# Grouping the state products of a state space stage: 512 moving columns instead of 256, and the stream sums added by accumulating transfers

## The chip, the cores and the metric

The kernel runs on one core of a Trainium2 chip. The metric is the device time of one execution in microseconds (us). The kernel before takes 2615.48 us (median of three runs, 2615.11 to 2616.11). All times below are of that core. PE is the matmul engine and PEld its weight load, DVE the vector engine, ACT the scalar engine, POOL the general engine, and SP the engine whose queue issues most of the loads.

## The reference

One layer for 256 frames of a new stream (the "prompt") and 16 frames for each of 8 running streams, so 384 rows in all, in float32. The part the change touches is the state space branch (64 heads of 64 columns in 8 groups, state size 128 per head):

```
xbc, new_conv = causal_conv(xbc, st_conv, conv_w, conv_b)      # 4 taps, SiLU
h, ys: per chunk
    y = einsum(cb * decay, xdt) + einsum(C, h) * exp(cum)      # C times the stored state
    h = h * exp(last) + einsum(B, w_end, xdt)                  # new state = decayed state + B x
a_ssd = gated_rmsnorm(y + d_skip * xh, z, ssd_norm)            # RMS over each group of 512 columns
```

Outputs are the two blocks of y and the new states; `new_ssm_prompt` (4 KB times 512, 2 MB) comes from the prompt product, `new_ssm_sample` (16 MB) is, per stream, the stored state times its decay plus the stream's own sum B x.

## The kernel before, in words

The whole kernel is one list of matmuls on PE. Every projection streams its weights from HBM: SP loads a 128x1024 block `w` (512 KB), ACT rounds it to the high part `wh` (line 72), DVE subtracts to get the low part `wl` (line 73), and PE does three matmuls of 384 columns for each of 8 blocks of the contraction (lines 100 to 102: `wh` by the high part of the activations, `wh` by their low part, `wl` by the high part). One such block is called a half here: 24 matmuls. A projection is two halves. `w`, `wh` and `wl` have three buffers each, so a half's split can begin only when PE has finished the half three places earlier, and it must end before PE comes to it.

The stage of the change (pools `phd` and `phd1`, from line 564) runs over 8 groups. A group has ten projections in this order: `BT`, `CT`, and four convolution inputs (all called `pj_x` in the profile), then four gates `z0` to `z3` (`pj_z`). Between the projections stand two blocks of small matmuls, called lumps here: the x lump after the third convolution input, and the z3 lump after `z3`. A group's 512 columns are worked on in two pairs of 256 columns; the x lump does the inner products of the first pair and the sums of the previous group's second pair, the z3 lump the other half. In a lump (names as in the profile):

- `t_pp` (line 693, `py<-xhl,Bhl`): the prompt's new state, six matmuls of 256 columns per pair. Its result shares a PSUM bank with `yi`, is copied by ACT (`pe`) and written.
- `t_trx` (650), `t_cb` (640), `t_trB` (634), `t_yT` (671): transposes and C B.
- `t_Y` (679): the outputs within the chunk, 48 rows of the trace per pair.
- `t_yi` (658, `py<-hs,Cm`): C times the stored states `hs`, eight matmuls of 256 columns per pair, shown as 16.
- `t_su` (798): B x of each stream, eight matmuls of 256 columns per pair. DVE then adds the result to the decayed `hs` (line 807, 64 adds), and one POOL transfer of 1 MB writes `new_ssm_s`.

Around the lumps ACT and DVE do the rest of the stage in their own order, mixed with the weight splits: the taps and SiLU of the convolution (`cbuf`, `cacc`, `xs`), the decay factors `E` (`eside`, exponentials and line 780), `hs` times its decay (`dside`), the gate `zs` (line 928), and the norm of the previous group (`final`, `finish`). For the norm ACT squares (`ysq`), POOL adds into `ssum` (line 836, one `ysq` buffer), ACT and DVE split the sum into `nh_g` and `nl_g` (lines 188, 189), and PE spreads it over the partitions by two matmuls with ones (`bc_g`, lines 192 and 193), which stand between `z1` and `z2`. ACT loads a function table (`ACT_TABLE_LOAD`) whenever the next function is not in the loaded one; exponentials and the SiLU functions alternate.

The order on each engine is set by a scheduler when the program is built. `lump` and `chain` only pin the order of PE's blocks; `later()` puts an instruction behind the last weight split. Engines run their lists strictly in order. After the stage come the last gate projections `gb` (their second half lies in this stage's end), with reloads `ar` of the branch's result (SP, line 966), which ACT and DVE split into `abh` and `abl` for the next stage's projections `sp`.

At the program's start SP loads the inputs `xw` in blocks; ACT and DVE split each into `xgh` and `xgl` and its first weights into `wh_e` and `wl_e`, and PE's first projection `pj_p` follows the arrivals.

## Time and profile before

| what | value |
|---|---|
| median of three runs | 2615.48 us |
| profiled execution | 2615.75 us, of which the span on the page is 2613.8 us |
| PE busy | 2602.6 us, 100% of the span |
| DVE, ACT, POOL busy | 1775.5, 1302.2, 185.7 us |
| PE's waits in the whole span | 1.2 us and 0.9 us, one each |
| granted clock of PE | 1.00 |
| state space stage | about 450 to 1205 us, one group every 90.0 us |

Busy shares are to be read with care here: matmuls overlap in the profile (a 384-column matmul is shown as 0.33 us long and the next one starts 0.163 us later), so what a block of matmuls takes is read from start to start. In rows of the trace in order of time the columns are: start (us from the span's start), length of the merged rows (us), engine, line, operation, result and sources, shape, count, and in brackets the idle time of the engine before, with what ended it.

### The profile page before, as it was taken

What the parts mean: (1) busy time and instruction counts of PE and PEld (TensorE: products, weight loads), DVE (VectorE), ACT (ScalarE), POOL (GpSimd) and SP (SyncE); (2) the same over time, 40 slices, a digit from 0 to 9 for tenths busy, and PEclk for the clock granted to TensorE, in tenths of its full rate; (3) what the DMA queues carried; (4) which work ended last, traced back from release to release, by engine and by line L of the source; (5) the groups of instructions that cost most, each with busy time, mean ns of one, the idle gap of its engine ahead of it and who ended that gap; (6) DMA issues with size and microseconds to landing.
All of it is one profiled execution on the core that took longest, in us unless ns stands there. A gap on an engine that the chain in (4) does not pass through costs nothing.

```text
span 2613.8 us, 40314 instructions
## 1 busy us (share of the span) xinstructions
PE 2602.6 (100%) x16001; PEld 2506.4 (96%) x16001; DVE 1775.5 (68%) x2383; ACT 1302.2 (50%) x1981; POOL 185.7 (7%) x264
## 2 busy tenths in 40 slices
PE   9999999999999999999999999999999999999998
PEld 9999999999999999999999988999999999999997
DVE  6685334788888888876434434766676868677677
ACT  6443325566566566744332334645454545454454
POOL 0000000001111111121000000000000000000000
PEclk9999999999999999999999999999999999999999
DMA  7444446566766676666654555533443444344343
GB/s 284 143 136 155 149 147 203 179 206 209 230 210 223 197 241 201 218 218 226 211 161 157 158 193 169 208 138 130 142 132 129 159 156 143 140 145 138 137 145 137
DMA packets 139421, 457.76 MB, mean 175 GB/s; under 512 B 17569, under 2 KB 44769, under 8 KB 125793
## 3 DMA queue, kind: packets, MB, share of 16 engines
q1 hardware_dynamic: 117120, 326.98, 39.0%
q0 software_dynamic: 22112, 128.21, 13.4%
q8 instruction: 126, 2.06, 0.3%
q14 instruction: 63, 0.51, 0.1%
HBM read 410.26 MB, written 44.86 MB: 174 GB/s over the span
## 4 chain that ended last, share of the span: by engine, by line
PE 98%; ACT 1%; DVE 1%; issue 0%; DMA 0%; POOL 0%; ACTq 0%; POOLq 0%
PE pj_up L100 6%; PE pj_up L101 6%; PE pj_up L102 6%; PE pj_x L100 4%; PE pj_x L102 4%; PE pj_x L101 4%; PE pj_sp L102 3%; PE pj_z L102 3%; PE pj_z L101 3%; PE pj_sp L100 3%; PE pj_sp L101 3%; PE pj_z L100 3%; PE X L1401 2%; PE c L1401 2%; PE X L1399 2%; PE c L1400 2%
## 5 line engine op out<-in xcount | busy, mean ns | idle before, releaser
L100 PE MATMUL pj_up<-x1h,wh_up 128*128 128x384 f32 (+1 forms) x1024 | 334.2, 326 | 0.0
L102 PE MATMUL pj_up<-x1h,wl_up 128*128 128x384 f32 (+1 forms) x1024 | 333.9, 326 | 0.0
L101 PE MATMUL pj_up<-x1l,wh_up 128*128 128x384 f32 (+1 forms) x1024 | 333.9, 326 | 0.0
L100 PE MATMUL pj_x<-xgh,wh_x 128*128 128x384 f32 x768 | 252.2, 328 | 0.0
L102 PE MATMUL pj_x<-xgh,wl_x 128*128 128x384 f32 x768 | 250.8, 327 | 0.9 <-DVE wl_x L73 0.9
L101 PE MATMUL pj_x<-xgl,wh_x 128*128 128x384 f32 x768 | 250.6, 326 | 0.0
L72 ACT ACTIVATE wh_up<-w_up 128x1024 fp32r<-128x1024 f32 x126 | 133.1, 1056 | 189.3 <-PE pj_up L101 114.7
L101 PEld LDWEIGHTS pj_up<-x1l,wh_up 128*128 128x128 f32 x1024 | 193.7, 189 | 0.4
L100 PEld LDWEIGHTS pj_up<-x1h,wh_up 128*128 128x128 f32 x1024 | 193.7, 189 | 0.4
L102 PEld LDWEIGHTS pj_up<-x1h,wl_up 128*128 128x128 f32 x1024 | 193.7, 189 | 0.0
L73 DVE TENSOR_TENSOR wl_up<-w_up,wh_up 128x1024 fp32r<-128x1024 f32 x126 | 153.7, 1220 | 57.9 <-ACT wh_up L72 57.0
L102 PE MATMUL pj_z<-xgh,wl_z 128*128 128x384 f32 x512 | 167.0, 326 | 0.0
L100 PE MATMUL pj_z<-xgh,wh_z 128*128 128x384 f32 x512 | 167.0, 326 | 0.0
L102 PE MATMUL pj_sp<-abh,wl_sp 128*128 128x384 f32 x512 | 167.0, 326 | 0.0
L101 PE MATMUL pj_z<-xgl,wh_z 128*128 128x384 f32 x512 | 167.0, 326 | 0.0
L100 PE MATMUL pj_sp<-abh,wh_sp 128*128 128x384 f32 x512 | 167.0, 326 | 0.0
L101 PE MATMUL pj_sp<-abl,wh_sp 128*128 128x384 f32 x512 | 167.0, 326 | 0.0
L73 DVE TENSOR_TENSOR wl_sp<-w_sp,wh_sp 128x1024 fp32r<-128x1024 f32 x64 | 78.3, 1224 | 116.6 <-ACT wh_sp L72 116.6
L72 ACT ACTIVATE wh_x<-w_x 128x1024 fp32r<-128x1024 f32 x96 | 101.0, 1052 | 107.1 <-PE pj_z L101 53.0
L73 DVE TENSOR_TENSOR wl_x<-w_x,wh_x 128x1024 fp32r<-128x1024 f32 x96 | 117.3, 1221 | 51.5 <-ACT wh_x L72 51.5
L72 ACT ACTIVATE wh_sp<-w_sp 128x1024 fp32r<-128x1024 f32 x64 | 67.8, 1059 | 166.3 <-PE pj_sp L101 158.2
L100 PEld LDWEIGHTS pj_x<-xgh,wh_x 128*128 128x128 f32 x768 | 145.3, 189 | 2.6 <-issue 0.4
(459 smaller groups left out, 7112.0 us busy)
## 6 DMA issues: line engine op xcount, KB each, us to landing
w_up<-w_up SPq DMA_DIRECT2D x128, 512.0 KB, 3.5
w<-w_dn POOLq DMA_DIRECT2D x60, 1024.0 KB, 5.2
w_x<-w_in SPq DMA_DIRECT2D x96, 512.0 KB, 4.1
w_z<-w_in SPq DMA_DIRECT2D x64, 512.0 KB, 3.6
w_sp<-w_ssd SPq DMA_DIRECT2D x64, 512.0 KB, 3.5
w_ga<-w_ga SPq DMA_DIRECT2D x32, 512.0 KB, 3.5
w_pp<-w_pp SPq DMA_DIRECT2D x32, 512.0 KB, 3.5
hs<-ssm POOLq DMA_DIRECT2D x16, 1024.0 KB, 6.8
```

The source lines that it names most:

```text
L72: cut[0] = s.activation(h, w, AF.Copy)
L73: cut[1] = v.tensor_tensor(l, w, h.bitcast(F32), ALU.subtract)
L100: te.matmul(out, wh, xh, start=first, stop=False, **how)
L101: te.matmul(out, wh, xl, start=False, stop=False, **how)
L102: return te.matmul(out, wl, xh, start=False, stop=last, **how)
L1399: te.matmul(o, h[:, t], vh, start=go, stop=False, skip_group_check=True)
L1400: te.matmul(o, h[:, t], vl, start=False, stop=False, skip_group_check=True)
L1401: last[0] = te.matmul(o, l[:, t], vh, start=False, stop=False, skip_group_check=True)
```

## The change

What was done for a pair of 256 columns is done for a group of 512:

- `t_pp`: six matmuls of 512 columns for a group, all in the x lump of the next group, in a PSUM bank of their own; one copy `pe` of 512 columns and one transfer of 256 KB instead of two of 128 KB.
- `t_yi`: eight matmuls of 512 columns for a group, all in its x lump; `hs` lies in two tiles of four streams each, loaded at the group's start, and `yis` is one operation of 512 columns (`yside`).
- `t_su`: two sets of four matmuls of 512 columns (`state(D, 0)` in the next x lump, `state(D, 1)` in the next z3 lump). The result is no longer added to `hs` by DVE. The decayed `hs` is written as it is (`dside`), and the sums are copied by ACT into `sst`, one of four copies behind each of the four halves after the lump (`spill`), and added to the written states in HBM by a transfer with `accum_op=ALU.add`.
- Buffers: `xst`, `sst`, `hs`, `Bhl`, `BT`, `CT` one each, `xs` five; the constant `ones` goes; `dynamic_dma_scratch_size=4096`.

```diff
@@ proj
             half(o, q, take(src, f"{name}_{q}"), rhs)
             if hook:
                 hook()
+            if spill:
+                with later():
+                    spill.pop(0)()
@@ pload, t_yi, t_pp
-        def pload(S):
-            S.hs = pd.tile([P, NB, 2 * P], F32, tag="hs", name=f"hs{S.nm}")
-            gp.dma_start(S.hs, io["ssm"][S.qd])
+        def pload(D):
+            D.hs = []
+            for k in range(2):
+                hs = pd.tile([P, 4, 512], F32, tag=f"hs{k}", name=f"hs{D.g}_{k}", bufs=1)
+                gp.dma_start(hs, io["ssm"][D.g, :, 4 * k : 4 * k + 4])
+                D.hs.append(hs)
...
-        def t_pp(S, py):
-            S.pp = py[:, :256]
+        def t_pp(D):
+            D.pp = mmtile(f"pp{D.g}")
...
+        def prompt(D):
+            lump(lambda: t_pp(D))
+            pe = pd.tile([P, 512], F32, tag="pe", name=f"pe{D.g}", bufs=1)
+            s.copy(pe, D.pp)
+            gp.dma_start(io["new_ssm_p"][D.g], pe)
@@ dside, state
+        def dside(D, k):
+            hs = D.hs[k].rearrange("p b (h q) -> p b h q", h=8)
+            dec = decb[:, D.g * 8 : D.g * 8 + 8, 4 * k : 4 * k + 4].rearrange("p h b -> p b h")
+            v.tensor_tensor(hs, hs, dec.unsqueeze(3).to_broadcast([P, 4, 8, 64]), ALU.mult)
+            gp.dma_start(io["new_ssm_s"][D.g, :, 4 * k : 4 * k + 4], D.hs[k])
+
+        def state(D, k):
+            su = []
             def t_su():
-                hs = S.hs.rearrange("p (r h) n -> p h r n", h=2)
-                for r2 in (0, 2):
...
-                        v.tensor_tensor(hr, hr, su[h].rearrange("p (r n) -> p r n", r=2), ALU.add)
+                for r in range(2):
+                    for h in range(2):
+                        t = slice(h * 64, h * 64 + 64)
+                        su.append(sstile(f"su{D.g}_{k}_{r}_{h}"))
+                        i = te.matmul(su[-1], D.bs[t, 2 * k + r, :], D.xst[t, 2 * k + r, :], start=True, stop=True)
                 return i
             lump(t_su)
-            gp.dma_start(io["new_ssm_s"][S.qd], S.hs)
+            sst = pd.tile([P, 4, 512], F32, tag="sst", name=f"sst{D.g}_{k}", bufs=1)
+            def out(i):
+                s.copy(sst[:, i], su[i])
+                if i == 3:
+                    gp.dma_start(io["new_ssm_s"][D.g, :, 4 * k : 4 * k + 4], sst, accum_op=ALU.add)
+            spill.extend([lambda i=i: out(i) for i in range(4)])
@@ the loop over groups, in the x lump
-            S.py = mmtile(f"py{S.nm}")
             if g:
-                lump(lambda: t_pp(prev.p[1], S.py))
+                prompt(prev)
...
-            lump(lambda: t_yi(S))
+            lump(lambda: t_yi(D))
             xside(S)
+            yside(D)
             mside(D)
             if g:
-                state(prev.p[1])
+                state(prev, 0)
@@ behind the z3 projection
-            lump(lambda: t_pp(S, S1.py))
             lump(lambda: t_trx(S1))
             lump(lambda: t_yT(S))
             lump(lambda: t_Y(S))
-            lump(lambda: t_yi(S1))
             xside(S1)
-            state(S)
+            if g:
+                state(prev, 1)
             final(S)
+            stack(D)
```

The scheduler gives the built program another order at three places that the prediction speaks of. In the rows a name's last number tells the tile apart; `wh_z_2_0` is the high part of the weights of the first half of `z2`, and a row without a result, `ACT_TABLE_LOAD`, loads a function table.

**ACT and PE between `z1` and `z2`** (third group of the loop; the other groups read alike). ACT before, from the split for the second half of `z1`:

```order
L72 ACTIVATE wh_z_1_1_7703<-w_z_1_1_7701 128x1024
L779 ACTIVATE E_0_7658<-E_0_7658 128x2x256
L188 ACTIVATE nh_g_7811<-ssum_7054 128x384
L593 COPY cbuf_4128<-cstate 128x8x3
L593 COPY cbuf_4130<-cstate 128x8x3
L607 ACT_TABLE_LOAD
L607 ACTIVATE xs_7656<-cacc_7651,vec 128x384
L928 ACTIVATE zs_0_7731<-zs_0_7731 128x384
L72 ACTIVATE wh_z_2_0_7750<-w_z_2_0_7748 128x1024
L72 ACTIVATE wh_z_2_1_7780<-w_z_2_1_7778 128x1024
```

and with the change, from the last of the four copies into `sst`, which stands right behind the split of the second half of `z1`:

```order
L819 COPY sst_0_7434<-su_0_1_1_7432 128x512
L609 ACT_TABLE_LOAD
L609 ACTIVATE xs_7525<-cacc_7520,vec 128x384
L794 ACT_TABLE_LOAD
L794 ACTIVATE E_0_7527<-E_0_7527 128x2x128
L936 ACT_TABLE_LOAD
L936 ACTIVATE zs_0_7603<-zs_0_7603 128x384
L795 ACT_TABLE_LOAD
L795 ACTIVATE E_0_7527<-E_0_7527 128x2x256
L71 ACTIVATE wh_z_2_0_7620<-w_z_2_0_7618 128x1024
L71 ACTIVATE wh_z_2_1_7650<-w_z_2_1_7648 128x1024
L190 ACTIVATE nh_g_7681<-ssum_6922 128x384
```

Two exponentials of `E` have moved behind the convolution's SiLU (`xs`) and around the gate's (`zs`), with a table load before each of the four, and `nh_g` has moved from behind the split of `z1` to behind both splits of `z2`. In the stretch from the x lump to `z2` ACT has seven table loads per group instead of four. On PE the two matmuls that use `nh_g` and `nl_g` stood together ahead of `z2`; with the change the rows from the last matmul of `z1` are:

```order
L101 MATMUL pj_z_1_7617<-xgh_495,wl_z_1_1_7574 128x384
L194 MATMUL bc_g_7685<-nh_g_7681,onesr 128x384
L99 MATMUL pj_z_2_7711<-xgh_230,wh_z_2_0_7620 128x384
L100 MATMUL pj_z_2_7711<-xgl_231,wh_z_2_0_7620 128x384
L195 MATMUL bc_g_7685<-nl_g_7682,onesr 128x384
L101 MATMUL pj_z_2_7711<-xgh_230,wl_z_2_0_7621 128x384
```

The first stays ahead of `z2` and the second has moved behind two of its matmuls.

**ACT at the program's start.** Before, the splits of the first inputs followed each other (`xgh`, `wh_e`, and so on); with the change:

```order
L273 ACTIVATE xgh_252<-xw_182,x0g 128x384
L295 ACTIVATE wh_e_249<-xw_182 128x256
L595 COPY cbuf_4118<-cstate 128x8x3
L595 COPY cbuf_4120<-cstate 128x8x3
L595 COPY cbuf_4122<-cstate 128x8x3
L273 ACTIVATE xgh_270<-xw_185,x0g 128x384
L297 ACTIVATE wh_e_274<-xw_185 128x512
```

Three copies of the state space stage's first convolution inputs have moved up to between the second and the third block of inputs. They need the transfer `cstate<-state_conv` (648 KB), which was issued by POOL at about 422 us and is now POOL's first transfer, behind its memsets and with nothing to wait for.

**SP behind the stage.** Before, with `ar` the reloads and `w_gb` the weights of the last gate projections:

```order
L65 DMA w_gb_1_12563<-w_gb 128x1024
L966 DMA ar_12798<-a_scr_72 128x384
L966 DMA ar_12804<-a_scr_73 128x384
L966 DMA ar_12840<-a_scr_74 128x384
L966 DMA ar_12846<-a_scr_75 128x384
L65 DMA w_gb_0_12598<-w_gb 128x1024
```

and with the change:

```order
L64 DMA w_gb_1_12715<-w_gb 128x1024
L973 DMA ar_12525<-a_scr_72 128x384
L973 DMA ar_12531<-a_scr_73 128x384
L973 DMA ar_12567<-a_scr_74 128x384
L973 DMA ar_12573<-a_scr_75 128x384
L64 DMA w_gb_0_12762<-w_gb 128x1024
L973 DMA ar_12614<-a_scr_76 128x384
```

The first four reloads have moved behind ten more weight blocks (before they were issued at 1170.7 us), and the first of them now also waits for the last accumulating transfer of `sst`, whose memory it takes.

More of the change, by code (lines that the diff above doesn't have):

```diff
@@ L49, in build @@
     ident = cst[:, C_IDENT : C_IDENT + P]
-    ones = cst[:, C_ONES : C_ONES + P]
     def mmtile(name):
@@ L115, in half @@
         last[0] = ins
-    queue, ready = [], []
+    queue, ready, spill = [], [], []
     def take(src, name):
@@ L203, in build @@
     b_scr = [dram.tile([P, 2, P], F32, name=f"b_scr{i}") for i in range(G)]
-    x_scr = [dram.tile([P, 2, 2, P], F32, name=f"x_scr{i}") for i in range(16)]
+    x_scr = [dram.tile([P, 2, 4, P], F32, name=f"x_scr{i}") for i in range(G)]
     x1_scr = [dram.tile([P, DM], F32, name=f"x1_scr{b}") for b in range(3)]
@@ L867, in build @@
                 eside(prev.p[1], 1)
-                dside(prev.p[1])
                 for i in range(4):
                     gate_b(i, pd, "cacc")
-                py = mmtile("pp_last")
-                lump(lambda: t_pp(prev.p[1], py))
+                prompt(prev)
                 lump(lambda: t_yT(prev.p[1]))
                 lump(lambda: t_Y(prev.p[1]))
-                state(prev.p[1])
+                state(prev, 0)
                 final(prev.p[1])
-                for i in range(4, 8):
+                for i in range(4, 6):
+                    gate_b(i, pd, "cacc")
+                state(prev, 1)
+                for i in range(6, 8):
                     gate_b(i, pd, "cacc")
@@ L936, in build @@
                 finish(prev)
+            dside(D, 0)
             zproj(2)
-            dside(S)
+            dside(D, 1)
             cload(D.p[1])
```

115 lines of the change are left out of this document (46 added, 69 removed).

## The prediction

> **What bounds the kernel now.** I read the page first, then PE's waits.
>
> ```profile
> span 2613.8 us, 40314 instructions
> PE warm_o L234 <- DVE warm L230: 1.2, 1, 1.2
> PE pj_x L102 <- DVE wl_x L73: 0.9, 1, 0.9
> ```
>
> PE stands still for 2.1 us in the whole span. So a microsecond saved on PE is a microsecond of the end, and a microsecond that PE waits anywhere is one too: nothing later can give it back. The question for every part of the change is whether PE's list gets shorter, and whether something PE needs now comes late. The next view is the busy time of each engine in one stretch of the stage, from an x lump to the norm's matmuls ahead of `z2` (columns: stretch, its length, then busy time and instruction count of PE, PEld, DVE, ACT, POOL, then clock, DMA share, GB/s).
>
> ```profile
> 635.00:666.00 31.00, 31.00 (x248) 29.79 (x247) 27.34 (x38) 24.48 (x48) 4.66 (x5) 1.00 0.68 228
> ```
>
> DVE has 3.7 us to spare here and ACT 6.5. Over the whole span both have plenty, but in this stretch work for ACT is nearly on the path, because the weight splits and `nh_g` stand in its list behind the rest.
>
> **PE's own work.** The lump rows in order of time, the first matmul after the lump, and the norm's first matmul:
>
> ```profile
> 635.49 0.88 PE L693 MATMUL py<-xhl,Bhl 128*128 128x256 f32 x6
> 636.21 0.82 PE L650 MATMUL trx<-cst,xs 128*128 128x128 f32 x6
> ...
> 640.14 1.08 PE L658 MATMUL py<-hs,Cm 128*32 128x256 f32 x16
> 641.15 0.75 PE L798 MATMUL su<-xst,bst 64*128 64x256 f32 x8
> 641.83 0.43 PE L100 MATMUL pj_x<-xgh,wh_x 128*128 128x384 f32 x1
> 665.34 0.34 PE L192 MATMUL bc_g<-nh_g,onesr 128*128 128x384 f32 x1
> ```
>
> From 641.83 to 665.34 lie six halves of 24 matmuls of 384 columns: 23.51 / 144 = 0.163 us each, so 512 columns take about 0.163 x 4/3 = 0.217 us. Six prompt matmuls of 256 columns take 0.72 us, 1.44 a group; six of 512 take 1.30. The 16 rows of `yi` run as four column groups at once, four rounds of 0.217 and 0.14 besides, 1.01 a pair and 2.02 a group; one set of 512 columns is four rounds of 0.434 and 0.14, 1.88. `su` is 0.68 a pair, four rounds of about 0.11 and 0.24 around them, 1.36 a group; two sets with two rounds of 0.217 and 0.2 around them make 1.27. Together 0.37 us less per group. Against it, in the z3 lump `yi` no longer stands between `Y` and `su`, so `Y` is followed by another tiling directly; I take 0.1 us for it. Eight groups, and one more lump at the end: about **-1.8 us**. Bounds: -0.5 (the fixed parts come back in full) and -4 (they vanish with the instructions). The columns streamed are the same; only fixed parts can go, so this term is small whatever happens.
>
> **ACT between the x lump and z2.** The change moves the state sums from DVE (64 adds) to ACT (64 copies), and the new order has seven table loads in this stretch of a group where there were four. Here every instruction of ACT's list counts. Rows of before, same group:
>
> ```profile
> 640.22 0.85 ACT L750 ACTIVATE xhl<-xdw 128x768 fp32r<-128x768 f32 x1 [1.46 <-DVE xdw L736]
> 641.09 1.28 ACT L768 ACT_TABLE_LOAD   x1
> 642.38 0.40 ACT L768 ACTIVATE E<-cbc,tok 128x128 f32<-128x128 f32 x1
> ...
> 643.23 0.69 ACT L770 ACTIVATE E<-cbc,tok 128x128 f32<-128x128 f32 x2
> 643.83 0.39 ACT L768 ACTIVATE E<-cbc,tok 128x128 f32<-128x128 f32 x1
> ...
> 645.00 0.41 ACT L778 ACTIVATE E<-E 128x256 f32<-128x256 f32 x1
> 645.30 0.62 ACT L779 ACTIVATE E<-E 128x512 f32<-128x512 f32 x1
> 645.82 0.39 ACT L768 ACTIVATE E<-cbc,tok 128x128 f32<-128x128 f32 x1
> 646.12 0.51 ACT L835 ACTIVATE ysq<-zs 128x384 f32<-128x384 f32 x1
> 646.53 1.05 ACT L72 ACTIVATE wh_z<-w_z 128x1024 fp32r<-128x1024 f32 x1
> 647.48 0.98 ACT L770 ACTIVATE E<-cbc,tok 128x128 f32<-128x128 f32 x3
> ...
> 654.56 0.24 ACT L594 COPY cbuf<-cbuf 128x45 f32<-128x45 f32 x1
> ...
> 655.36 1.05 ACT L72 ACTIVATE wh_z<-w_z 128x1024 fp32r<-128x1024 f32 x1
> ...
> 656.83 0.51 ACT L188 ACTIVATE nh_g<-ssum 128x384 fp32r<-128x384 f32 x1
> ...
> 660.14 0.52 ACT L928 ACTIVATE zs<-zs 128x384 f32<-128x384 f32 x1 [0.65 <-DVE zs L927]
> 660.57 1.99 ACT L72 ACTIVATE wh_z<-w_z 128x1024 fp32r<-128x1024 f32 x2
> ```
>
> From start to start: `xhl` 0.87, a table load 1.29, an `E` of 128 columns 0.30, the exponential pair 0.30 + 0.52 = 0.82, `ysq` 0.41, a split 0.95, the convolution's three (654.56 to 655.36) 0.80, `zs` 0.43; `xs`, of the same size, 0.5. A copy into `sst` is in no row. Its floor is the 0.30 of a 256-column operation, its ceiling the 0.62 of a 512-column one; I take 0.47, near the 0.52 at which the 512-column row lets the next one start.
>
> With the change the list from `xhl` to `nh_g` is: `xhl` 0.9, 7 table loads 9.0, 16 `E` 4.8, 2 exponential pairs 1.6, 2 `ysq` 0.8, 4 `sst` 1.9, 5 splits (`z0_1` to `z2_1`) 4.8, the convolution's three 0.8, 2 `xs` 1.0, `zs` 0.4, `nh_g` 0.5: **26.5 us without one wait**. `xhl` starts 4.7 us into the lump (640.22 - 635.49); the longer prompt product need not move that, since DVE is at a split until then. So `nh_g` is ready no sooner than 31.2. PE comes to `bc_g` after a lump of 6.34 + 0.58 (prompt) + 0.87 (`yi`) - 0.04 = 7.75 and six halves of 23.5: at **31.25**. Before, `nh_g` was ready at 21.9 (656.83 + 0.51 - 635.49) and PE used it at 29.85: a cover of 8 us that is now zero before any wait is counted.
>
> There are waits. The second `ysq` needs the only buffer, which POOL's add frees:
>
> ```profile
> 601.75 4.70 POOL L836 TENSOR_TENSOR ssum<-ssum,ysq 128x384 f32<-128x384 f32 x1 [0.75 <-ACT ysq L835]
> 646.71 1.05 POOL L836 TENSOR_TENSOR ssum<-ssum,ysq 128x384 f32<-128x384 f32 x1 [0.97 <-ACT ysq L835]
> 649.82 2.01 POOL L836 TENSOR_TENSOR ssum<-ssum,ysq 128x384 f32<-128x384 f32 x1 [2.06 <-ACT ysq L835]
> ```
>
> Before, six `E` and a split stood between the two `ysq`; now only a `sst` copy and one `E`, 0.8 us. By the middle duration ACT waits 2.01 + 0.1 + 0.05 - 0.8, about 1.4 us (0.4 by the shortest, 4 by the longest), and 0.6 before the first `ysq`, whose gate product DVE finishes about 8 us into the lump. So `nh_g` is ready at about 33.2: PE waits **2.0 us** at `bc_g`. Behind it DVE's list decides:
>
> ```profile
> 649.76 1.21 DVE L780 TENSOR_TENSOR E<-E,cbm 128x1024 f32<-128x1024 f32 x1
> 660.02 0.55 DVE L189 TENSOR_TENSOR nl_g<-ssum,nh_g 128x384 fp32r<-128x384 f32 x1
> 661.64 2.36 DVE L73 TENSOR_TENSOR wl_z<-w_z,wh_z 128x1024 fp32r<-128x1024 f32 x2 [1.07 <-ACT wh_z L72]
> ```
>
> The last exponential ends 2.4 us (two splits and `nh_g`) before `nh_g`, at 30.8; then come 1.21 for `E`, 2.36 for the two low parts and 0.55 for `nl_g`, ready at 35.0. PE, having passed two matmuls of `z2`, would be at the second `bc_g` at 33.2 + 0.5 = 33.7 and waits another **1.3**. So 3.4 us per group, and seven groups have a previous one: **+24 us**. Bounds: with no wait inside ACT's list 1.4 us per group, +10; with POOL's longest add and `sst` at 0.62 about 6.6, +46. What follows in a group has time to recover, as ACT waits for PE's buffers from `z3` on, so the wait does not grow from group to group.
>
> On the table loads the Trainium skill speaks against the change still more: "ScalarE: Activation LUTs", "What ACT_TABLE_LOAD costs", gives 1283 ns for the load and about 1380 ns of drain, 2.66 us a switch. The trace has the 1.28, but the next instruction starts 1.29 us after the load began, so there is no drain here; by the page, as an estimate, each group would lose some 10 us more.
>
> **The opening.** POOL now sends 648 KB at once into the time in which the inputs arrive:
>
> ```profile
> 5.00:10.00 5.00, 5.00 (x27) 4.95 (x27) 3.53 (x8) 3.26 (x7) 0.00 (x0) 1.00 1.03 397
> cstate<-state_conv POOLq DMA_DIRECT2D x1, 648.0 KB, 7.5
> 10.97 0.62 ACT L271 ACTIVATE xgh<-xw,x0g 128x384 fp32r<-128x384 f32 x1 [0.52 <-DMA xw<-xw]
> 13.43 0.33 PE L101 MATMUL pj_p<-xgl,wh_e 128*128 128x384 f32 x1
> 13.84 0.43 PE L102 MATMUL pj_p<-xgh,wl_e 128*128 128x384 f32 x1
> ```
>
> The DMA share is 1.03 at 397 GB/s, so 648 KB (664 thousand bytes) more put the inputs behind it back by 1.6 us. PE already waited for the block that came at 10.97 (a step of 0.41 instead of 0.16), so the delay is paid in full. The three copies ahead of `xgh` in ACT's list wait for the same transfer: issued at about 1 us and 7.5 us under way, it lands at 8.5, 0.2 us a copy, about as late as the delayed input. **+1.6 us**, bounds 0.5 (the transfer fills gaps) and 4 (it lands later, and ACT with it).
>
> **Behind the stage.** The first reloads `ar` now stand ten weight blocks later in SP's list, and ACT's list has splits of `gb` behind `abh`, which wait for them.
>
> ```profile
> new_ssm_s<-hs POOLq DMA_DIRECT2D x16, 1024.0 KB, 5.0
> hs<-ssm POOLq DMA_DIRECT2D x16, 1024.0 KB, 6.8
> ar<-a_scr SPq DMA_DIRECT2D x32, 192.0 KB, 4.5
> ```
>
> Each reload takes 4.5 us to land; with two or four of them ahead of a split, and two halves (7.8 us) between its release and its use, one or two splits of `gb12` come 1 to 2 us late: **+3 us**, bounds 0 and 9. SP comes to the first `ar` about 11 us after the last accumulating transfer is issued. That transfer is in no row: at least the 5.0 of the plain write, at most, if it reads and writes one after the other, 11.8. I take 8, which hides.
>
> **Sum**, against the profiled execution's own 2615.75 us (0.3 above the median): 2615.75 - 1.8 + 24 + 1.6 + 3 = **2643**.
>
> **Rivals.** *ACT keeps up* (not slower): POOL's add takes its short 1.05 and the copies 0.3, and the overlaps on ACT are a little better than my sum; then the waits at `bc_g` vanish and -1.8 and +1.6 remain: 2615.5. It speaks for it that ACT had 6.5 us free in the stretch; against it that three loads, four copies and the new wait take 3.9 + 1.9 + 2.0 = 7.8, and that it takes off only the part of ACT's list that is in front of the last exponential, while DVE's tail of 4.1 us stays. *A partial form*, 1.4 us a group or less: 2620 to 2630. *The accumulating transfer is slow*: from 11 us on, the first `ar` holds SP, with the weight blocks behind it; at 20 us the end moves by 20 - 11 = 9 and about 4 for the reloads behind it: 2656. Nothing in the trace excludes it. *The clock falls*: PE now stands 2.0 and 1.3 us, nearly at a stretch, in each of seven groups. If the clock were halved for the half behind each, 3.9 us more per group: 2643 + 27 = 2670. The granted clock was 1.00 in all stretches I looked at, but none had a wait over 1.2 us. The Trainium skill, "TensorE: Matmul & The Clock Gate", Part 1, has the clock fall after an idle window of about 3.4 us; two matmuls lie between the waits, so by that rule it could go either way.
>
> **How the numbers follow.** Forecast 0.64 (its own range 2630 to 2656), partial 0.10, ACT keeps up 0.06, slow transfer 0.11, clock 0.09. The range 2626 to 2662 leaves out ACT keeping up, the clock, and a part of the partial and slow-transfer cases. A measurement of this kernel tells about 0.2% (5.2 us) from no change. Slower by more: everything but ACT keeping up and the edge of the partial case, 0.93; within 0.2%: 0.04; faster: 0.03, only if ACT keeps up and PE's fixed parts vanish.
>
> **What would show it.** Right: PE's waits list `bc_g` on ACT's `nh_g` and on DVE's `nl_g`, seven times each, 2 and 1.3 us, and the groups take about 93 us instead of 90.0; ACT is busy nearly all the time from the x lump to `z2`. PE's first projection ends 1 to 2 us later; `pj_gb` waits for `wh_gb` once or twice. Wrong: no wait at `bc_g`, or a wait at a weight split elsewhere in the stage; a granted clock under 1; `ar` waiting for `sst`.

## The result, and the profile after

The changed kernel takes **2662.5 us** (median of six, 2660.0 to 2667.5); the kernel before took 2615.9 on the same chip. The ratio is **1.018**, 95% interval 1.0169 to 1.0195: slower, as forecast, but by 46.6 us where 27 were expected; the forecast was 2643 and its range ended at 2662. The profiled execution took 2662.4 us, 2660.7 of it inside the span.

First PE's waits on the page of the kernel after (total us, times, longest):

```profile
span 2660.7 us, 39759 instructions
PE bc_g L194 <- ACT nh_g L190: 9.0, 7, 1.5
PE bc_g L195 <- DVE nl_g L191: 5.7, 7, 0.9
PE su L812 <- DVE xdw L746: 4.8, 8, 1.6
PE pj_p L313 <- ACT xgh L273: 3.2, 1, 3.2
PE pj_gb L99 <- ACT wh_gb L71: 1.1, 1, 1.1
PE pj_x L99 <- ACT wh_x L71: 1.1, 1, 1.1
```

The two waits at `bc_g` are there, seven times each. The third row, `su` behind DVE's eviction `xdw`, was in no forecast. Now one group in the order of time, ACT, DVE and PE around the norm:

```profile
576.94 1.28 ACT L936 ACT_TABLE_LOAD   x1
...
578.78 1.28 ACT L795 ACT_TABLE_LOAD   x1
...
580.61 1.99 ACT L71 ACTIVATE wh_z<-w_z 128x1024 fp32r<-128x1024 f32 x2
582.50 0.51 ACT L190 ACTIVATE nh_g<-ssum 128x384 fp32r<-128x384 f32 x1
583.07 0.45 PE L194 MATMUL bc_g<-nh_g,onesr 128*128 128x384 f32 x1 [1.19 <-ACT nh_g L190]
584.15 0.55 DVE L191 TENSOR_TENSOR nl_g<-ssum,nh_g 128x384 fp32r<-128x384 f32 x1
584.75 0.69 PE L195 MATMUL bc_g<-nl_g,onesr 128*128 128x384 f32 x1 [0.91 <-DVE nl_g L191]
585.24 0.52 PE L101 MATMUL pj_z<-xgh,wl_z 128*128 128x384 f32 x1
585.55 0.53 PE L99 MATMUL pj_z<-xgh,wh_z 128*128 128x384 f32 x1
...
588.24 0.33 PE L99 MATMUL pj_z<-xgh,wh_z 128*128 128x384 f32 x1
```

ACT has no idle time from 576.94 to 583.0: two table loads with the gate and an exponential behind them, two splits, then `nh_g`. PE stands 1.19 us for it, runs two matmuls, stands 0.91 us for `nl_g`, and after that each matmul of 384 columns takes 0.32 us from start to start, twice the usual 0.163, until the last row. The same place in stretches (length, busy time and count of PE, PEld, DVE, ACT, POOL, clock, DMA share, GB/s):

```profile
580.00:584.70 4.70, 2.65 (x15) 2.05 (x13) 3.97 (x5) 3.22 (x7) 0.55 (x1) 0.99 1.09 257
584.70:588.20 3.50, 3.45 (x11) 3.45 (x12) 1.02 (x2) 0.00 (x0) 0.00 (x0) 0.52 0.97 356
588.20:591.70 3.50, 3.50 (x24) 3.50 (x23) 0.81 (x1) 1.89 (x2) 0.00 (x0) 1.00 1.00 414
```

The granted clock falls to 0.52 for one stretch and returns. PE counts as busy all the while, so the waits list does not show this loss; the start-to-start steps do. Up to the end of PE's work there are nine such patches, some 87 matmuls at half speed, which cost 13.5 us. The profile also shows the lump behind `z3`, where the new wait for `su` stands, and what came before it on ACT and DVE:

```profile
970.84 1.06 ACT L71 ACTIVATE wh_z<-w_z 128x1024 fp32r<-128x1024 f32 x1 [6.54 <-DMA w_z<-w_in]
971.93 1.23 DVE L72 TENSOR_TENSOR wl_z<-w_z,wh_z 128x1024 fp32r<-128x1024 f32 x1 [5.37 <-ACT wh_z L71]
...
981.26 0.82 PE L655 MATMUL trx<-cst,xs 128*128 128x128 f32 x6
...
982.27 2.35 DVE L72 TENSOR_TENSOR wl_x<-w_x,wh_x 128x1024 fp32r<-128x1024 f32 x2
984.10 0.50 PE L812 MATMUL su<-xst,bst 64*128 64x512 f32 x2
985.48 0.54 DVE L746 TENSOR_TENSOR xdw<-trx,tok 128x384 f32<-128x384 f32 x1
986.17 0.46 PE L812 MATMUL su<-xst,bst 64*128 64x512 f32 x1 [1.56 <-DVE xdw L746]
```

The third `su` needs the PSUM bank in which the transposes `trx` lie until DVE has evicted them (`xdw`), and DVE comes to it late. The chain begins at a late weight block: ACT stands 6.54 us until `w_z` has landed, DVE 5.37 us for ACT's split of it, and from 971.93 on DVE works without a pause, two weight splits of 2.35 us at the end, until it reaches `xdw`. Start to start these lumps take 3.5 to 6.3 us, 8.6 us over seven times 3.50. Last the transfers of after (KB each, median us to landing), three of them as they were before, and the opening of after in the order of time:

```profile
new_ssm_s<-sst POOLq DMA_DIRECT2D x16, 1024.0 KB, 11.6
hs<-ssm POOLq DMA_DIRECT2D x16, 1024.0 KB, 8.7
w_x<-w_in SPq DMA_DIRECT2D x96, 512.0 KB, 5.2
w_z<-w_in SPq DMA_DIRECT2D x64, 512.0 KB, 4.4
xw<-xw SPq DMA_DIRECT2D x1, 320.0 KB, 7.6
```

```profile
w_x<-w_in SPq DMA_DIRECT2D x96, 512.0 KB, 4.1
w_z<-w_in SPq DMA_DIRECT2D x64, 512.0 KB, 3.6
xw<-xw SPq DMA_DIRECT2D x1, 320.0 KB, 4.2
```

```profile
1.31 0.67 POOL L570 DMA_DIRECT2D cstate<-state_conv  x1 [0.36 <-issue]
9.30 0.61 ACT L273 ACTIVATE xgh<-xw,x0g 128x384 fp32r<-128x384 f32 x1 [4.69 <-DMA xw<-xw]
9.97 0.92 PE L313 MATMUL pj_p<-xgh,wh_e 128*128 128x384 f32 x4 [3.25 <-ACT xgh L273]
```

The accumulating transfer takes 11.6 us. `w_x` and `w_z` land 1.1 and 0.8 us later than before, and ACT's waits for `w_z`, which the list of before does not show at all, come to 41.8 us. At the start the second block of inputs (320 KB) landed 3.4 us later than before, and PE stood 3.25 us for it.

All of it, from start to start on PE, in the two profiled executions (spans 2613.8 and 2660.7, a difference of 46.9):

| where | forecast | measured |
|---|---|---|
| PE's own small matmuls | -1.8 | -0.8 |
| waits at `bc_g`, seven groups | +24 | +19 |
| opening | +1.6 | +4.0 (1.5 of it at half clock) |
| late weights at the start of the stage and in `gb` | +3 | about +3.6 |
| waits at `su`, z3 lumps | 0 | +8.6 |
| half clock outside the opening | 0 (a rival) | +12.0 |
| sum | +26.8 | +46.4 |

From `sp` on the two kernels take the same time. The stretch from the stage's first matmul to `sp`'s, called the stage below, went from 846.9 to 889.6 us.

### The profile page after: what moved, and what is told of

Read it like the earlier page. It is cut to its first block, busy times and chain, and to the rows that moved or that the text cites. A ratio compares the mean times of both kernels' runs of the same rounds, so it can differ in the third digit from the quotient of the medians.

```text
span 2660.7 us, 39759 instructions
## 1 busy us (share of the span) xinstructions
PE 2624.0 (99%) x15761; PEld 2509.4 (94%) x15761; DVE 1736.7 (65%) x2311; ACT 1367.9 (51%) x2065; POOL 172.8 (6%) x272
## 3 DMA queue, kind: packets, MB, share of 16 engines
q0 software_dynamic: 24288, 144.99, 16.3%
## 4 chain that ended last, share of the span: by engine, by line
PE 94%; DVE 3%; ACT 1%; DMA 1%; issue 1%; POOL 0%; SPq 0%; DVEq 0%; ACTq 0%
PE pj_up L99 6%; PE pj_up L100 6%; PE pj_up L101 6%; PE pj_x L99 5%; PE pj_x L101 5%; PE pj_x L100 5%; PE pj_sp L100 3%; PE pj_sp L99 3%; PE pj_sp L101 3%; PE pj_z L99 2%; PE pj_z L101 2%; PE pj_z L100 2%; PE X L1408 2%; PE c L1408 2%; PE c L1406 2%; PE X L1407 2%
## 5 line engine op out<-in xcount | busy, mean ns | idle before, releaser
L101 PEld LDWEIGHTS pj_x<-xgh,wl_x 128*128 128x128 f32 x768 | 146.0, 190 | 1.0 <-DVE wl_x L72 1.0
```

What stands on the lines that cost most here:

```text
L101: return te.matmul(out, wl, xh, start=False, stop=last, **how)
```

## The experiments

The theory: ACT's list got seven table loads per group instead of four, because the copies into `sst` changed the scheduler's order, and so `nh_g` and the splits of `z2` come late; idle PE then loses its clock. The rivals: the copies themselves, the accumulating transfer, the larger loads and the opening.

**The opening undone.** `cstate` is queued behind `mlast`, the last write of the stage before into `ma_scr`.

```diff
-        gp.dma_start(cst_, io["state_conv"])
+        with behind(mlast[0]):
+            gp.dma_start(cst_, io["state_conv"])
```

> The changed kernel with one edit: the transfer of the stored convolution states is queued on POOL behind the last write of the pool branch, so that it and its three copies on ACT leave the opening. Theory (the transfer holds the input blocks up, and ACT and PE behind them): PE's first projection loses its 3.2 us wait and the cold matmuls behind it, the first gate projection starts at 53.0 us instead of 57.0, and the whole is 4.0 us shorter, about 2658.5. The state space stage keeps its seven waits at bc_g. Rival (the opening is slow for another reason, such as a longer load of the program): the 4 us stay.

Measured 2658.3 us, 1.016 (1.0143 to 1.0177): 4.2 less than the change. `pj_ga` begins at 53.7 instead of 57.0, and the waits at `bc_g` and `su` stay (9.1, 6.0 and 5.1). So the time came out as the theory said (2658.5): the opening costs 3 to 4 us and nothing else hangs on it.

**The factors early.** `eside(S, 1)` is written ahead of `zproj(0)`; copies, accumulating transfer and opening stay.

```diff
-            zproj(0)
             eside(S, 1)
+            zproj(0)
```

> The changed kernel with one line moved: the second half of the decay factors of a group's first pair is written ahead of the projection z0 instead of behind it. ACT's list then has four table loads between the x lump and z2 instead of seven; the 64 copies on ACT, the accumulating transfers and the opening stay. Theory (ACT's list with its table loads makes nh_g and the split of z2 late, and the clock falls behind the waits): the waits at bc_g vanish, by the rows' durations about 0.8 us per group remain at a split of z1, and the clock falls seldom; the part from the first convolution projection to the first pj_sp takes 847 (before) + 7 + up to 5 = 854 to 862 us, the whole 2630 to 2638. Rival one (the 64 copies on ACT alone make it late, whatever the tables): waits of 2 us or more per group stay, the whole above 2645. Rival two (the accumulating transfers slow the weights' loads): the whole stays at 2655 to 2662.

Measured 2630.5 us, 1.0054 (1.0039 to 1.0069), within the 2630 to 2638 of the theory. Between 545 and 1100 us ACT has 36 table loads (60 with the change, 38 before), no wait at `bc_g` is left, and no patch of half clock in the stage. So the order of ACT's list, and not the time of the copies, made the waits at `bc_g`: with the patches behind them and what they pushed, 32 us. Waits at `su` remain (2.5 us), and 14 us over the kernel before.

**The norm's split early.** All seven table loads stay; only `nh_g` and `nl_g` move ahead of `z0`.

```diff
+            if g:
+                prev.hl = norm_split(pd, prev.ssum, f"g{prev.g}")
             zproj(0)
             eside(S, 1)
```

> The changed kernel with the split of the norm's sum (nh_g on ACT, nl_g on DVE) written ahead of the projection z0, so that both stand well ahead of the splits of z2. ACT still has seven table loads per group in this stretch. Theory (the length of ACT's list is what counts, the place of nh_g only says which wait shows it): no wait at bc_g, in its place a wait of about 2 us per group at the splits of z2; 13 us less than that for the bc_g waits saved at most; the whole 2645 to 2658. Rival (the place of nh_g is the cause): no waits over 0.5 us in the groups, the whole at 2625 or less.

Measured 2644.2 us, 1.0109 (1.0094 to 1.0125), 18 less than the change and just below the 2645 to 2658 expected. The wait moved, as PE's waits show:

```profile
PE pj_z L99 <- ACT wh_z L71: 6.6, 7, 1.0
PE pj_z L101 <- DVE wl_z L72: 6.0, 7, 0.9
```

PE now waits for the splits of `z2`, behind which `nh_g` had stood. So the late work is the whole list up to `z2`; `nh_g` was only the last of it: the waits were 14.7 us at `bc_g` and are 12.6 here. The rest of what the move brought lies behind the waits. In the profiled execution (2648.2 us) three patches of half clock are left outside the opening instead of eight, and the z3 lumps take 3.7 us over seven times 3.50 instead of 8.6.

**The copies on DVE.** ACT's list then has four table loads again.

```diff
-                s.copy(sst[:, i], su[i])
+                v.tensor_copy(sst[:, i], su[i])
```

> The changed kernel with the 64 copies of the stream sums on DVE instead of ACT. The accumulating transfers and the early transfer in the opening stay; ACT's list is back at four table loads per group, as before the change. Theory: no waits at bc_g and none at su, the clock stays at 1.00 in the stage; the opening's 4.0 and about 3 to 5 us of waits in the last gate projections remain, less 0.8 on PE: 2621 to 2625. Rival (the accumulating transfers, which read and write the states in HBM, slow the loads): the waits stay at weights that land late, the whole above 2640.

Measured 2632.2 us, 1.0068 (1.0051 to 1.0084), 7 to 11 more than expected. The `bc_g` waits went, as they should, but `su` still waits (3.8 us, six times), and ACT waits 69.2 us for `w_z` to land. The stage takes 859.0, 12 more than before. With this the theory was short of a cause: something that neither ACT's list nor the opening explains, and that comes with the transfers.

**The three together, and then the transfers.** A base without the list and without the opening: copies on DVE, `cstate` late, and `sst` in another pool, with three later pools in another order, so that memory shared by the stages lies elsewhere.

```diff
-            sst = pd.tile([P, 4, 512], F32, tag="sst", name=f"sst{D.g}_{k}", bufs=1)
+            sst = pd1.tile([P, 4, 512], F32, tag="sst", name=f"sst{D.g}_{k}", bufs=1)
```

> The changed kernel with three edits: the copies of the stream sums on DVE, the transfer of the convolution states back behind the pool branch, and the memory of the stage behind arranged so that the first reloads ar are issued two weight blocks earlier (sst in the stage's second pool, the pool of gbt allocated first). Theory: the opening's 4 us and the waits at bc_g and in the last gate projections go; what stays are the waits at su in the z3 lump, about 7 to 9 us with the cold matmuls behind them, and -0.8 of PE's own work: 2621 to 2626. Rival (nothing but the table loads and the opening mattered): 2615.

Measured 2630.6 us, 1.006 (1.0046 to 1.0074): above the 2621 to 2626 expected, with the stage at 859.6 and `su` waiting 4.6 us. Two kernels on this base then each changed the transfers alone. In the first the loads of the next group's states are queued behind `alast`, the norm's last write into `a_scr`, so that they no longer run in the middle of the gates:

```diff
-                gp.dma_start(hs, io["ssm"][D.g, :, 4 * k : 4 * k + 4])
+                with behind(alast[0]):
+                    gp.dma_start(hs, io["ssm"][D.g, :, 4 * k : 4 * k + 4])
```

> The run best with one more edit: the two loads of the next group's stored states (1 MB each) are queued on POOL behind the four writes of the branch's result, which come with z3, instead of right behind the writes of the decayed states. Theory (several megabytes of states moved in one stretch make weight blocks of z2 and z3 land late, DVE then does the splits and the norm late, and the evictions that su waits for come late): the ACT waits for w_z and the su waits shrink to under half, 2616 to 2620. Rival (the su waits come from DVE's own list alone, with the norm's chain ahead of the evictions): no change against best.

Measured 2618.6 us, 1.001 (1.0001 to 1.0019). PE's waits:

```profile
PE pj_x L101 <- DVE wl_x L72: 2.0, 3, 0.9
```

No wait at `su`, all z3 lumps 3.5 us from start to start, the stage 848.4. It is 0.1% over before (0.01 to 0.19), and not faster. The accumulating transfer, 10.3 us here, is still there. Late blocks are still there too, at another place: `w_x` takes 6.8 us to land where the base had 5.3, and ACT waits 33.8 us for `w_x` instead of 16.0, and 34.3 for `w_z` instead of 59.6. In this kernel PE hardly notices it. In the second kernel `sst` is written without adding, over the decayed states; it leaves out the sum, so that the new stream states are incomplete.

```diff
-                    gp.dma_start(io["new_ssm_s"][D.g, :, 4 * k : 4 * k + 4], sst, accum_op=ALU.add)
+                    gp.dma_start(io["new_ssm_s"][D.g, :, 4 * k : 4 * k + 4], sst)
```

> The run best with the sums written plainly over the decayed states instead of added, so the new stream states are left incomplete: 16 MB less is read in the stage, all else and every order the same. Theory (load of the DMA queues): the transfers of sst take 5 to 6 us instead of 11.6, the weights land earlier and the su waits fall, 2 to 5 us less than best. Rival (they wait for DVE only): the same as best within 1 us.

Measured 2619.6 us, 1.0013 (1.0004 to 1.0022). That is 11.0 less than the base, where 2 to 5 were expected. The transfer lands in 6.7 us instead of 10.8, `su` waits 1.9 us, the stage takes 851.0. So either remedy alone takes away three quarters or more of the 14.6 us that the base had over before: on this base it takes both, the accumulation and the loads in one stretch, to make weights late enough to cost that much.

**The loads alone in the changed kernel.**

> The changed kernel with one edit, the one of best_hl: the two loads of the next group's stored states wait on POOL for the four writes of the branch's result. ACT's list and every other order stay as in the changed kernel. Theory (two separate causes: ACT's list makes bc_g late, and the states' transfers make weight blocks late, which shows at su): the waits at bc_g stay within 2 us of 9.0 and 5.7 in sum, with cold matmuls behind most of them; the waits at su (4.8) fall under 2; the whole 2650 to 2657. Rival (the transfers are the larger cause even of the bc_g waits): bc_g under 8 in sum and the whole under 2645.

The edit is that of the loads above, and all else is as in the changed kernel. Measured 2653.2 us, 1.0144 (1.0128 to 1.0161), within the expected range. The waits at `su` are gone altogether, as expected. The first waits at `bc_g` should have stayed within 2 us of 9.0, and grew to 12.1; half clock was expected behind most of them, and came in three of the seven groups:

```profile
PE bc_g L194 <- ACT nh_g L190: 12.1, 7, 2.7
PE bc_g L195 <- DVE nl_g L191: 6.5, 7, 0.9
```

The growth lies in three groups, with waits of 2.7, 1.9 and 2.7 us; the other four wait 1.1 to 1.4, as they did with the change (1.2 to 1.5). ACT's list is as long as it was, but in these three groups it begins late. ACT stands 4.2 to 4.5 us for a block `w_x`, whose split then begins 15.5 to 16.3 us ahead of the lump's first `yi` (16.8 or more in the other groups), and `xhl`, with which the list begins, starts 0.7 to 1.6 us later after that `yi` than in the changed kernel. One of the three:

```profile
816.94 1.06 ACT L71 ACTIVATE wh_x<-w_x 128x1024 fp32r<-128x1024 f32 x1 [4.45 <-DMA w_x<-w_in]
...
832.89 0.84 ACT L759 ACTIVATE xhl<-xdw 128x768 fp32r<-128x768 f32 x1 [1.24 <-DVE xdw L749]
```

So the late loads cured `su` and made other blocks late. With the change ACT waits 41.8 us for `w_z` and 13.2 for `w_x`, here 10.4 and 32.3, and `w_x` takes 7.0 us to land instead of 5.2.

**All three undone, copies and accumulation kept.** Factors early, `cstate` late, loads late.

> The change with three causes undone together and the ACT copies and accumulating transfers kept: the second half of the decay factors written ahead of z0 (four table loads a group again), the transfer cstate queued behind the a-branch, and the next group's stored states queued behind the last a_scr writes. If the list of ACT, the opening and the bunched loads of the stored states are all there is, the three effects add: 2662.5 - 31.9 (factors) - 4.2 (cstate) and the 5 to 7 us of waits for su and weights that were left in the kernel with early factors: 2619 to 2622, no wait over 1 us at bc_g or su, no patch of half clock in the stage. If ACT's copies or the accumulating transfers cost something of their own beside these, waits at pj_z for wl_z or wh_z stay in nearly every group and the time stays at 2624 to 2628. Below 2614 neither holds.

Measured 2634.2 us, 1.0065 (1.0051 to 1.0079): above both ranges, and 3.6 over the kernel with early factors alone. The effects do not add. Neither `bc_g` nor `su` waits, but PE waits for a split of `z0`, in all seven groups:

```profile
PE pj_z L101 <- DVE wl_z L72: 7.2, 7, 1.3
PE pj_x L101 <- DVE wl_x L72: 2.9, 4, 0.9
PE pj_x L99 <- ACT wh_x L71: 1.5, 3, 0.7
```

ACT's list in such a group, from the split for the first half of `z0` to that for its second:

```profile
1021.19 1.04 ACT L71 ACTIVATE wh_z<-w_z 128x1024 fp32r<-128x1024 f32 x1
1022.13 0.56 ACT L823 COPY sst<-su 128x512 f32<-128x512 f32 x1
...
1029.52 1.04 ACT L71 ACTIVATE wh_z<-w_z 128x1024 fp32r<-128x1024 f32 x1
```

They are 8.3 us apart, and PE needs a half every 3.9 us. With early factors alone the two lie as far apart, and PE waits for the second 0.2 us in six groups. Here, in six of the seven groups, the first of them comes 0.5 to 1.7 us later, counted from the lump's first `yi`, and the wait in these is 0.7 to 1.3 us. What the rows show ahead of it is the same as in the kernel before this one: ACT has stood 3.0 to 4.4 us for a block `w_x`, whose split begins 15.3 to 16.5 us ahead of `yi` (`w_x` takes 7.3 us to land, 6.7 with early factors alone). With early factors alone that split begins 17.6 us ahead or earlier, except in one group (16.2), and that group waits 1.0 us at `z0` too. Of the 8.3 us one copy into `sst` is 0.5; the rest is the order. With the copies on DVE the scheduler's list has the two splits 5.5 us apart, with two table loads between them as here, and no split of `z` waits although `w_x` is late there too (the first kernel with late loads above). So the transfers decide when ACT's list begins, and its order decides whether PE feels it. What a copy on ACT costs by itself, and whether the late `w_x` is all of the 3.6 us, no run separates.

**The price of a wait by itself.** Three kernels are the kernel before with copies on POOL of the norm's low part ahead of the second `bc_g`, 0.55 us each; nothing else changes. In the first two the number of copies is 4 + g and 9 + g in group g.

```diff
         v.tensor_tensor(l, sumsq, h.bitcast(F32), ALU.subtract)
+        for c in range(dose[0]):
+            gp.tensor_copy(l, l)
```

> The kernel before with a wait of growing length put in at bc_g: between nl_g and its use POOL copies the tile onto itself, 4 times in the first group and one time more in each group behind it, about 1 us each. PE then waits at bc_g from 0 to about 6 us in steps of about 1 us. Theory (an idle stretch of PE over a certain length makes the granted clock fall for some 3 us, and shorter ones do so only now and then): no cold matmuls behind the waits under 1 us, always behind those over 4 us, about 10 matmuls of 0.32 us start to start each time. Rival (the cold stretches in the changed kernel have another cause, such as the load of the DMA queues): no cold matmuls behind any of them.

> The run dose with longer waits: 9 copies on POOL in the first group and one more in each behind it, 0.55 us each, so by dose's own steps PE waits about 2.2, 2.8, 3.3, 3.9, 4.4, 5.0 and 5.5 us in groups 0 to 6 and little in the last. Theory (a stretch of about one to two windows of some 3 us decides, where the wait falls in the window matters): cold matmuls behind one or two of the three shortest and behind all from 3.9 us on, 10 to 11 each at twice the step. Rival (any wait over 2 us does it): behind all seven. Rival two (only several waits close together do it): behind none.

With 4 + g: 2626.7 us (one execution). The copies took half of the 1 us expected, so the waits above 4 us come only in the second kernel. The waits in the last five groups come to 8.4 us from start to start, and only the longest (2.68 us) is followed by a patch, ten matmuls, 1.6 us: 10.0 of the 10.6 us measured. With 9 + g: 2652.7 us (one execution), waits of 1.90, 2.48, 3.04, 3.53, 4.19, 4.75 and 5.32 us, 27.5 in all from start to start, and patches behind the last five, 8.8 us more than in before: 36.3 of 36.6. One of the three shortest has a patch and all from 3.53 us on, as expected; that any wait over 2 us brings one is out, since 2.48 did not. A wait costs itself, and a patch some 1.6 us, whatever the wait's length. But no length divides the cases: after the change, waits of 1.19 and 0.91 with two matmuls between them brought a patch (583 us, above), and with late loads the same pair did not:

```profile
582.21 0.44 PE L194 MATMUL bc_g<-nh_g,onesr 128*128 128x384 f32 x1 [1.18 <-ACT nh_g L190]
583.91 0.44 PE L195 MATMUL bc_g<-nl_g,onesr 128*128 128x384 f32 x1 [0.93 <-DVE nl_g L191]
```

In the changed kernel the times at which the nine patches end (the first at 14.60, the last at 1287.77) are whole multiples of 3.4133 us apart: counted from the first, they lie at 0, 127, 168, 196, 224, 252, 286, 308 and 373 times that, within 0.02. A stretch of 3.4133 us is called a window from here on. That suggested a fixed grid, and a last kernel with ten copies in every group was made for it:

> The kernel before with ten copies of the norm's low part on POOL in each of the eight groups, so that the second bc_g waits for the same time, 2.3 to 2.8 us, in each of the seven groups that come ahead of z2. Theory of a window: the clock is decided on a fixed grid of 3.413 us that runs through the whole execution; a window in which PE stands for about 1.9 us or more is followed by one at half clock. Then equal waits give unequal results, some of the seven with a patch of half clock and some without (by the share of phases at which 1.9 us of a 2.5 us wait fall in one window, about six in ten: three to five of seven), all patches end at the same phase of 3.413 us (within 0.1 us), and the idle time within the window separates the ones with a patch (1.9 us or more) from those without (1.8 or less). Theory of a length: the length of a wait decides, from about 2.5 us on; then all seven have a patch or none has. In time: 7 waits of about 2.4 us and 1.6 us per patch, 2615.9 + 17 + 5 to 8 = 2638 to 2641 by the first; 2633 or 2644 by the second.

Measured 2640.2 us (one execution), inside the 2638 to 2641 of the theory of a window. The seven waits are equal and the outcome is not; three of them, and the stretch behind each:

```profile
578.01 0.44 PE L197 MATMUL bc_g<-nl_g,onesr 128*128 128x384 f32 x1 [2.51 <-POOL nl_g L193]
670.79 0.45 PE L197 MATMUL bc_g<-nl_g,onesr 128*128 128x384 f32 x1 [2.50 <-POOL nl_g L193]
858.03 0.45 PE L197 MATMUL bc_g<-nl_g,onesr 128*128 128x384 f32 x1 [2.50 <-POOL nl_g L193]
```

```profile
580.00:582.80 2.80, 2.80 (x19) 2.80 (x18) 2.12 (x5) 0.53 (x1) 0.00 (x0) 1.00 0.45 165
672.00:675.20 3.20, 3.20 (x12) 3.20 (x11) 2.91 (x5) 0.00 (x0) 0.00 (x0) 0.50 0.34 95
859.50:862.70 3.20, 3.20 (x22) 3.20 (x20) 2.65 (x5) 0.40 (x1) 0.00 (x0) 1.00 0.40 129
```

Behind the waits that end at 670.79, 950.81 and 1138.16 the clock is 0.50, behind the four others 1.00. The three patches end at 675.23, 955.11 and 1142.85, worked out from the steps between the rows: 279.88 and 187.74 apart, 82.00 and 55.00 times 3.4133. Laid on that grid, the idle time within one window is 2.37, 2.50 and 2.12 us ahead of the three patches and at most 1.88 elsewhere, a little over the 1.8 expected. The theory of a length is out.

## Why the prediction was right or wrong, point by point

- **The table loads and `nh_g`: right.** The step "ACT between the x lump and z2" is borne out, line by line: seven loads, `nh_g` behind the splits of `z2`, first ACT and then DVE late. The size was 24 us (at 3.4 a group, though 2.0 and 1.3 make 3.3) and is 19, since PE waits 1.2 instead of 2.0 us for `nh_g` and 0.9 instead of 1.3 for `nl_g`. That it came so close is in part luck. In the group shown the list has every instruction that was counted, but takes 27.5 us without its waits at `ysq`, not 26.5; the waits are 0.4 and 0.5 us, not 0.6 and 1.4; and `xhl` starts 4.2 us into the lump, not 4.7. Early factors took away the waits, as the step demands.
- **The clock: the step that failed most.** It stood among the rivals with a chance of 0.09, because no stretch looked at had shown a clock under 1.00, and those had no wait over 1.2 us. That was an argument from rows that could not show it. Two waits of 2.1 us together can lie in one window of 3.41 us, and five of seven groups were hit. That it was five is in part luck of the phase: seven equal waits of 2.5 us, put into the kernel before, brought three. Its price was taken as 3.9 us a group, a whole half; a patch is one window and costs 1.6. Outside the opening it came to 12.0 us.
- **"That transfer ... I take 8, which hides": failed.** The accumulating transfer takes 11.6 us, next to the upper bound of 11.8 and over the 11 from which the rival on `ar` was to decide. That rival's place was wrong too: the last transfer, 11.8 us long, had landed 3.2 us before SP came to the first `ar`. The transfer, together with the loads of `hs`, hits the weights of the stage instead, and DVE's splits, and through them a PSUM bank at `su`: 8.6 us that no step had. Moving the loads brought this wait to zero in all three kernels that did it, though it made `w_x` late in its place.
- **`yi` out of the z3 lump: one side was not seen.** The step priced only the change of tiling (0.1 us). `yi` had also given DVE about 1 us between `Y` and `su` to evict `trx`; without it `su` meets the bank still full as soon as DVE is late. That DVE's lateness and not this alone is the cause follows from the late loads, where the same order has no wait.
- **The opening: the mechanism right, the term too small.** The block of inputs was late by 3.4 us, not by the 1.6 worked out from bytes over GB/s (664 / 397 is nearer 1.7), and the wait of 3.25 us brought a patch of 1.5 us. The measured 4.0 is the upper bound.
- **PE's own work: -0.8 instead of -1.8.** The prompt's six matmuls take 1.39 us, not 1.30, and `Y` ahead of `su` 1.87 instead of 1.76. The change has less than 1 us to win on PE in all, so even with every side effect gone it could win no more than that. No kernel here has them all gone; the nearest, the late loads on the base, is 2.5 us over before.
- **Behind the stage:** 3 forecast, 3.6 together with the waits at the start of the stage; `gb` itself waited 1.1 and 0.7 us.

The sum was 20 us short: 2.4 (opening), 12.0 (clock), 8.6 (`su`), 0.6 (weights) and 1.0 (PE's work) too little, 5 (`bc_g`) too much. The term that was forecast and the one that was only a rival are not two cases of which one comes true. The patches follow from waits, so a share of them belonged into the sum and not beside it.

## What to carry to other kernels

When a change gives an in-order engine more instructions, read its whole list in the new order, table loads included; here another order with the same copies on ACT was worth 32 us, and taking the copies off ACT no more than that (2630.5 and 2632.2 us). When PE is the bound, price every forecast wait with what follows it: here 1.6 us of half clock more whenever about 2 us of idle time fall into one window of 3.41 us. And do not add up what single remedies bring: the loads that were moved away from one set of weight blocks made another set late, and three remedies together brought less than one of them.

## What the runs showed of the hardware that was not expected

**The clock is decided on a free-running grid.** In six profiled executions with three patches or more, all 32 patches end on a grid of 3.4133 us (the period that fits best in each of them), with another phase in every execution. Between 440 and 1300 us a patch followed every window in which PE stood 2.0 us or more, and none in which it stood less than 1.8, but for a patch already under way; between them lie cases of both kinds (1.89 and 1.93 with, 1.88 and 1.97 without). The idle times are worked out from start-to-start steps and are good to about 0.1 us. The granted clock that the traces record, apart from these steps, has the same patches: each 3.41 us long, one of 6.83, and in each of the six executions their starts are whole numbers of windows apart. A patch lasts one window as a rule, in which some ten matmuls of 384 columns take 0.32 us each; the patch behind the wait of 4.75 us went on into a second window, 17 matmuls in all, though PE stood only 1.1 us in the first. A loop whose period is a whole number of windows repeats its luck: in the changed kernel four patches in a row end 95.57 us, or 28.00 windows, apart. The Trainium skill, "TensorE: Matmul & The Clock Gate", Part 1, has this window, 3413 ns and free-running, and the traces agree with both; where it asks for an idle window before the clock falls, they show that somewhat less than 60% of a window is enough.

**An accumulating transfer took much longer than a plain write.** On the same base 1 MB from SBUF added to HBM took 10.8 us, and the plain write that stood in its place 6.7; in the changed kernel it took 11.6 beside 6.2 for the plain write of the decayed states. That it costs its read and its write one after the other is not shown: in the changed kernel these take 8.7 and 6.2 us by themselves. The weight blocks of another queue landed later than before in the same stretch (3.6 to 4.4, and 4.1 to 5.2 us), but most of that is not the accumulation: without it they took 4.3 and 4.6 us, with it 4.7 and 5.3, on the same base.

**A large transfer on one queue delayed a smaller one on another by more than its bytes.** 648 KB issued by POOL at 1.3 us put a block of 320 KB, issued by SP at 1.66 us, back by 3.4 us; at the 397 GB/s at which the opening ran before, its bytes are worth 1.7. In the five kernels with this order the block took 7.3 to 8.0 us to land, and 3.9 to 4.5 in the nine that issue the 648 KB later.
